# Hyena mixer: first loads in another order, and the last second-gate projections woven beside the long convolutions

## The chip, the core and the metric

One core of a Trainium2 chip runs the whole program once. The metric is device time in microseconds (us) of one execution. The engines that work on their own queues are PE (matrix products), DVE (vector), ACT (activations, casts, copies), POOL (a second, slower vector engine) and SP (which here only issues transfers). Each takes its instructions strictly in the order of its queue and waits on semaphores of the others.

## What is computed

Two blocks follow each other on a sequence of 512 positions and 1024 channels. The first has four layers, with mixers hyena, window attention, pooling, hyena, and a SwiGLU feed-forward behind each; the second is a gated delta network beside latent attention. The change lies for the most part in the first Hyena mixer, which is also the first work of the program:

```python
def hyena_mixer(xn, w_in, b_in, conv_w, conv_b, fw1, ..., w_out, b_out):
    u = short_conv(xn @ w_in + b_in)          # 3 x 1024 channels: x1, x2 (gates) and v
    kf = rfft(hyena_filters(...))             # sine MLP of 3 layers, a decay, a normaliser
    v = x1 * long_conv(v, kf[order 0])        # through a DFT
    v = x2 * long_conv(v, kf[order 1])
    return v @ w_out + b_out
```

(This is the reference cut down; xn is the RMS norm of x.) The normaliser is the sum of absolute filter values over time.

## The kernel before, in words

Everything is fp32, and a product of fp32 matrices is made of three matmuls on high and low parts (L384, L385, L386). A **part** is one projection of 128 output channels: 8 blocks of the contraction by 3 matmuls, so 24 matmuls of 128x512 into one PSUM bank. Its weights come as a raw tile `wraw` (L350), ACT casts the high half `whi` (L372) and DVE makes the low half `wlo` (L373).

The work of a stage is written as Python generators. `weave` (L205) takes, again and again, the next piece of the stream that has done the smallest share of its declared total, so the numbers `HY_IN`, `HY_F`, `HY_P` in line 232 set how the instructions of two streams lie between each other in each engine's queue. The queues are fixed when the program is built; nothing is reordered on the chip.

The first Hyena mixer runs in three stretches.

- **Start.** SP loads the eight tiles of x (L274), then weights, the DFT matrix `fwd` (L610) and the filter MLP's inputs (L556 to L566). ACT squares x (L446, L449), DVE adds the squares up (L450), PE sums over channels (L453), ACT and DVE make 1/rms (L456, L459). The filter MLP (`filter_mlp`, L553) is three small matmuls (L571), each followed by a chain of seven vector operations and a sine on ACT (L538 to L550).
- **Filters beside inputs.** `inputs` makes the 24 parts of w_in: four channel blocks q of 256 channels, three kinds (2 is v, 0 the first gate, 1 the second gate), two parts each. The evicted part is scaled, short-convolved (`short`: L790 on DVE, L792 on ACT, two L794 on DVE), transposed on PE (L802, not for kind 1) and stored to the DRAM tile `vd` by POOL (L806). Beside it `filters` makes eight filters (four blocks by two orders). Each has 16 matmuls L653, the normaliser (L665, `kacc` summed by POOL L661), the scaling (L667 to L672), the folds on POOL (L585, L586) and DVE (L595, L596), 16 DFT matmuls (L605), the scaling into K (L684), and a store of K to the DRAM tile `kd` by POOL (L689). The trace has two records for each matmul of the DFTs, their inverses and L665.
- **Convolutions.** `hyena_conv` runs two chains, blocks 0 and 2, blocks 1 and 3. Each order of a block loads K (L850), folds v on POOL, does 16 DFT matmuls (L605), the products with K on DVE and POOL, and 16 inverse matmuls (L863 or L871). The output projection `out` (L384 to L386, from `acth`) begins when two blocks are through.

The second Hyena mixer makes its filters earlier, in another stage, and projects its inputs beside its convolutions.

Waits that the change touches: a convolution of block q starts when all inputs of block q are there (`given[0] <= q`), and the SP queue loads K after POOL's stores that used the same memory before.

Of the kernel before, what the change touches and what calls it, by code (L numbers as in the profile page):

```python
# [15 lines left out]
P = 128  # L16
D = 1024
T = 512
KD = D // P
# [212 lines left out]
HY_Q, HY_IN, HY_F, HY_P = 4, 125.0, 140.0, 125.0  # L232
# [4 lines left out]
class Builder:  # L237
    def __init__(self, ctx, tc, i, o):
# [13 lines left out]
        self.open_x(i["xT"])  # L252
# [15 lines left out]
    def open_x(self, src):  # L268
# [3 lines left out]
        self.xsum, self.xsums = None, 0  # L272
        for k in range(KD):
            self.nc.sync.dma_start(out=self.x[k], in_=src[k * P:(k + 1) * P, :])  # L274
# [278 lines left out]
    def filter_mlp(self, tl, s):  # L553
        nc, i = self.nc, self.i
        z = tl([P, T], "sh")
        nc.sync.dma_start(out=z[:66, :], in_=i["c_z"])  # L556
        vf = tl([P, 4], "vf")
        nc.sync.dma_start(out=vf, in_=i["vf"][:, 4 * s:4 * s + 4])
        ws = []
        for j in range(3):  # L560
# [3 lines left out]
            for d in range(2):  # L564
                src = i["hy_f_w1"][s] if j == 0 else i["hy_f_wi"][s, j - 1]
                nc.sync.dma_start(out=w[kk * d:kk * d + kk, 64 * d:64 * d + 64], in_=src)  # L566
            ws.append(w)
        h, kk = z, 66
        for j in range(3):
# [4 lines left out]
            yield 8.0  # L574
# [38 lines left out]
    def filters(self, pool, s, ctl=None, nk=1):  # L613
# [133 lines left out]
    def hyena(self, li, s):  # L747
        self.vd = self.dram.tile([4, 3, P, 1024], F32, name=self.nm("vd"))
        with self.pool("hd") as dp:
            tl = self.tl(dp)  # L750
            with self.pool("hp") as pool:
                first = None
                if s in self.kd:
                    inputs = self.hyena_in(pool, pool, li, s)
                    self.fwd = self.load_dft(tl, "fwd")
                else:
                    with self.pool("hf") as fp:
                        inputs = self.hyena_in(pool, fp, li, s)
                        weave((inputs(0, HY_Q), HY_IN), (self.filters(fp, s, tl, 2), HY_F))
                        first = [tl([P, 4, 256], f"first{k}") for k in (2, 0)]  # L760
                        for t, k in zip(first, (2, 0)):
                            self.nc.sync.dma_start(out=t, in_=self.vd[0, k].rearrange("p (a c) -> p a c", a=4))
                if first is None:
                    with self.pool("hy") as pool:
                        self.hyena_conv(pool, s, first, inputs)
            if first is not None:
                with self.pool("hy") as pool:
                    self.hyena_conv(pool, s, first, inputs)
# [1305 lines left out]
```

## Time and profile before

| what | value |
|---|---|
| median of 3 runs | 4196.17 us (4184.2 to 4198.35) |
| profiled execution | 4197.38 us |
| its span | 4195.6 us |
| mean granted clock of PE | 0.966 of full speed |
| PE busy | 3970.3 us, 95% of the span |
| DVE, ACT, POOL busy | 60%, 37%, 23% |

The span is the time from the first to the last instruction; 1.8 us lie around it. A busy matmul row is not a matmul at full speed: the clock that the throttle grants PE has two levels, and at the lower one the same matmul takes about twice as long. So a stretch is read by three things together: how much of it PE was busy, at which clock, and what ended the idle time before an instruction (the releaser, behind `<-`).

### The profile page before, as it was taken

The numbers are of one execution on the slowest core, as the hardware profiler recorded it, in microseconds if no ns is written. First come the engines' busy times: TensorE is split into PE (matmuls) and PEld (weight loads), VectorE is DVE, ScalarE is ACT, GpSimd is POOL, SyncE is SP. The second block draws the span as 40 slices with busy tenths as digits, with TensorE's granted clock in tenths as the row PEclk, the third lists the DMA queues.
The fourth block names the chain that finished last, engine by engine and source line by source line (L and its number), as shares of the span: only waits on it lengthen the run. The fifth ranks groups of instructions, "written<-read, shape, count | busy, mean of one in ns | idle before, by whom it ended". The sixth has DMA issues, their size and how long they took to land. (4 is left out here: it accounts for less than half of the span.)

```text
span 4195.6 us, 48459 instructions
## 1 busy us (share of the span) xinstructions
PE 3970.3 (95%) x18340; PEld 3207.3 (76%) x18340; DVE 2502.2 (60%) x4113; ACT 1564.7 (37%) x2859; POOL 979.7 (23%) x1031
## 2 busy tenths in 40 slices
PE   7988999999999999999998999979999999999999
PEld 5777788876788777877877788768888876677887
DVE  6756887467634465556666544567767665644333
ACT  4321322258522352323222322454544456743222
POOL 2544211021101112323333110123333321102111
PEclk8999999999999999999999999989989989999999
DMA  4542355230232233434431323311112111242322
GB/s 155 171 175 97 101 190 191 86 108 31 71 100 92 83 106 119 132 117 151 154 123 63 100 93 99 94 56 51 56 59 63 56 45 45 91 136 81 100 91 91
DMA packets 370771, 421.83 MB, mean 101 GB/s; under 512 B 20614, under 2 KB 337046, under 8 KB 365674
## 3 DMA queue, kind: packets, MB, share of 16 engines
q1 hardware_dynamic: 361514, 377.46, 28.4%
q0 software_dynamic: 8736, 40.93, 2.6%
q8 instruction: 144, 2.36, 0.2%
q14 instruction: 89, 0.73, 0.1%
q10 hardware_dynamic: 288, 0.34, 0.0%
HBM read 372.27 MB, written 44.32 MB: 99 GB/s over the span
## 5 line engine op out<-in xcount | busy, mean ns | idle before, releaser
L372 ACT CAST whi<-wraw 128x1024 fp32r<-128x1024 f32 (+4 forms) x546 | 533.1, 977 | 1383.5 <-PE ps L385 1235.4
L384 PE MATMUL ps<-xh,whi 128*128 128x512 f32 x1904 | 784.8, 412 | 15.0 <-ACT whi L372 15.0
L373 DVE TENSOR_TENSOR wlo<-wraw,whi 128x1024 fp32r<-128x1024 f32 (+4 forms) x546 | 673.2, 1233 | 194.0 <-ACT whi L372 174.4
L386 PE MATMUL ps<-xh,wlo 128*128 128x512 f32 x1904 | 758.6, 399 | 2.5 <-DVE wlo L373 2.3
L385 PE MATMUL ps<-xl,whi 128*128 128x512 f32 x1904 | 755.2, 397 | 0.5 <-DVE xl L471 0.5
L384 PEld LDWEIGHTS ps<-xh,whi 128*128 128x128 f32 x1904 | 359.8, 189 | 99.7 <-ACT whi L372 15.5
L386 PEld LDWEIGHTS ps<-xh,wlo 128*128 128x128 f32 x1904 | 359.0, 189 | 94.0 <-DVE wlo L373 5.5
L385 PEld LDWEIGHTS ps<-xl,whi 128*128 128x128 f32 x1904 | 359.9, 189 | 88.2 <-issue 3.8
L527 POOL TENSOR_TENSOR u<-u,a 128x512 f32<-128x512 f32 x88 | 154.3, 1756 | 1011.2 <-ACT whi L372 720.7
L384 PE MATMUL ps<-hh,whi 128*128 128x512 f32 x960 | 385.0, 401 | 3.0 <-ACT hh L312 3.0
L386 PE MATMUL ps<-hh,wlo 128*128 128x512 f32 x960 | 380.6, 397 | 1.1 <-DVE wlo L373 1.1
L385 PE MATMUL ps<-hl,whi 128*128 128x512 f32 x960 | 380.2, 396 | 1.0 <-DVE hl L313 1.0
L384 PE MATMUL ps<-act,whi 128*128 128x512 f32 x656 | 278.4, 424 | 0.2 <-ACT whi L372 0.2
L386 PE MATMUL ps<-act,wlo 128*128 128x512 f32 x656 | 272.3, 415 | 0.5 <-DVE wlo L373 0.5
L385 PE MATMUL ps<-act,whi 128*128 128x512 f32 x656 | 272.5, 415 | 0.0
L384 PEld LDWEIGHTS ps<-hh,whi 128*128 128x128 f32 x960 | 181.2, 189 | 46.4 <-ACT hh L312 4.7
L386 PEld LDWEIGHTS ps<-hh,wlo 128*128 128x128 f32 x960 | 181.0, 189 | 45.3 <-DVE wlo L373 2.0
L385 PEld LDWEIGHTS ps<-hl,whi 128*128 128x128 f32 x960 | 181.2, 189 | 45.0 <-DVE hl L313 2.4
L532 DVE TENSOR_TENSOR x<-x,ps 128x512 f32<-128x512 f32 x128 | 87.7, 685 | 198.2 <-PE ps L386 197.8
L605 PE MATMUL ps<-pg,fwd 128*128 128x256 f32 x512 | 133.5, 409 | 30.1 <-DVE pg L595 30.1
L386 PEld LDWEIGHTS ps<-act,wlo 128*128 128x128 f32 x656 | 129.6, 197 | 29.9 <-DVE wlo L373 1.0
L385 PEld LDWEIGHTS ps<-act,whi 128*128 128x128 f32 x656 | 129.6, 198 | 25.1 <-issue 0.5
(539 smaller groups left out, 7238.7 us busy)
## 6 DMA issues: line engine op xcount, KB each, us to landing
wraw<-ff_w_gate SPq DMA_DIRECT2D x44, 1024.0 KB
wraw<-ff_w_up SPq DMA_DIRECT2D x44, 1024.0 KB
wraw<-ff_w_down SPq DMA_DIRECT2D x32, 1024.0 KB
wraw<-w_in SPq DMA_DIRECT2D x53, 512.0 KB
wraw<-hy_w_in SPq DMA_DIRECT2D x24, 1024.0 KB
w<-w_mod SPq DMA_DIRECT2D x24, 1024.0 KB
kd<-K POOLq DMA_DIRECT2D x16, 1152.0 KB, 4.7
K<-kd SPq DMA_DIRECT2D x16, 1152.0 KB
```

The source lines that it names most:

```text
L372: nc.scalar.copy(out=hi, in_=src)
L373: nc.vector.tensor_tensor(out=lo, in0=src, in1=hi.bitcast(F32), op=SUB)
L384: nc.tensor.matmul(out[:m, :cols], lhsT=whi[:, k, :m], rhs=xhi[:, :cols], start=(first and k == 0), stop=False)
L385: nc.tensor.matmul(out[:m, :cols], lhsT=whi[:, k, :m], rhs=xlo[:, :cols], start=False, stop=False)
L386: nc.tensor.matmul(out[:m, :cols], lhsT=wlo[:, k, :m], rhs=xhi[:, :cols], start=False, stop=(last and k == nk - 1))
L527: nc.gpsimd.tensor_tensor(out=u, in0=u, in1=a, op=MUL)
L532: self.nc.vector.tensor_tensor(out=self.x[j], in0=self.x[j], in1=ps, op=ADD)
L605: nc.tensor.matmul(ps[:, c, :], lhsT=self.fwd[:, t, s, c, :], rhs=st[t][s], start=(s == 0), stop=(s == 1))
```

## The change

- **Start.** The loads of x are split off from the tiles' allocation (`load_x`). In the first mixer the filter MLP is started first (`next(filters)`), and for it the MLP's loads go out on ACT's queue. Then come the first weight tile, now in two halves of 128 columns, the eight loads of x, and the other weights; `fwd` is loaded after the MLP's inputs. The squares go through `final(k)`: ACT squares, POOL adds (one buffer `xsq`), DVE adds the last.
- **Inputs.** Kind 1 of blocks 2 and 3 (two items, four parts, 96 matmuls) is taken out of the filter stretch and made by the stream `project` beside the convolutions, with a total of `HY_LATE` = 60. A convolution waits only for the items it needs. `HY_IN` goes from 125 to 104, `HY_F` from 140 to 148, the MLP's piece from 8 to 20.
- **Delay.** The eviction and short convolution of a part (`take`) is written one part later, in both Hyena mixers, and with it the transposes.
- **Second block.** One weight of the weave at the start of the delta network goes from 30 to 20.

The diff, cut:

```diff
-HY_Q, HY_IN, HY_F, HY_P = 4, 125.0, 140.0, 125.0
+LATE, HY_LATE = (2,3), 60.0
+HY_Q, HY_IN, HY_F, HY_P = 4, 104.0, 148, 125.0
...
     def filter_mlp(self, tl, s):
         nc, i = self.nc, self.i
+        q = nc.sync if s else nc.scalar
         z = tl([P, T], "sh")
-        nc.sync.dma_start(out=z[:66, :], in_=i["c_z"])
+        q.dma_start(out=z[:66, :], in_=i["c_z"])
...
-            yield 8.0
+            yield 20.0 if s == 0 else 8.0
...
+        yield from self.filter_mlp(tl, s)
         self.fwd = self.load_dft(ctl, "fwd")
-        yield from self.filter_mlp(tl, s)
...
-                self.want_cols(w, 0, KD, (kind * 8 + q * 2) * P, 256)
+                if s or kind != 1 or q not in LATE:
+                    self.want_cols(w, 0, KD, (kind * 8 + q * 2) * P, 256, 256 if self.plan else P)
+        for q in () if s else LATE:
+            self.want_cols(w, 0, KD, (8 + q * 2) * P, 256)
...
+            early = [(q, k) for q in range(4) for k in (2, 0, 1) if k != 1 or q not in LATE]
+            with self.pool("hp") as pool, self.pool("hf") as fp:
+                filters = self.filters(fp, s, tl, 2)
+                next(filters)
+                self.load(0)
+                self.load_x(self.i["xT"])
+                self.ahead()
+                inputs = self.hyena_in(dp, pool, fp, li, s)
+                for k in range(KD):
+                    self.final(k)
+                weave((inputs(early), HY_IN), (filters, HY_F))
...
+            with self.pool("hp2") as pool, self.pool("hy") as hy:
+                self.in_tiles = self.tl(pool)
+                self.hyena_conv(hy, s, first, inputs, [(q, 1) for q in LATE])
...
+        def inputs(items):
+            for q, kind in items:
+                st = self.in_tiles([P, 1024], "st", 2)
+
+                def consume(j, ps):
+                    given.append((j, ps, q, kind, st))
+                    if len(given) > 1:
+                        take(*given.pop(0))
+                yield from self.proj(2, xs, consume)
+            take(*given.pop())
+            turn(*waiting.pop())
...
-            while given[0] <= q:
+            while missing & {(q, 2), (q, 0)}:
                 yield 0.5
...
                 if order:
+                    while (q, 1) in missing:
+                        yield 0.5
...
-        weave((chain(conv(0), conv(2)), 76.0), (chain(conv(1, 12.0), conv(3)), 88.0), (out(0), 70.0), (project(), HY_P))
+        weave((chain(conv(0), conv(2)), 76.0), (chain(conv(1, 12.0), conv(3)), 88.0), (out(0), 70.0), (project(), HY_LATE if first else HY_P))
...
-        weave((self.gate_scalars(b2, lambda: tl([P, 6, P], "w", 7).rearrange("p c d -> p (c d)"), given[0], sc), 30),
+        weave((self.gate_scalars(b2, lambda: tl([P, 6, P], "w", 7).rearrange("p c d -> p (c d)"), given[0], sc), 20.0),
```

What this does to the queues stands below at two places; the names are those of the program, and the line numbers of the changed kernel are some 3 to 20 higher.

ACT's queue at the start, before:

```order
L254 DMA vecs<-vecs 128x542
L256 DMA ident<-c_ident 128x128
L446 ACT_TABLE_LOAD
L446 ACTIVATE tmp_221<-x_72 128x512
L470 ACTIVATE xh_108<-x_72,vecs 128x512
```

and in the changed kernel:

```order
L255 DMA vecs<-vecs 128x542
L257 DMA ident<-c_ident 128x128
L560 DMA sh_101<-c_z 66x512
L562 DMA vf_103<-vf 128x4
L570 DMA fw_19_105<-hy_f_w 33x64 x2
L570 DMA fw_20_109<-hy_f_wi 64x64 x2
L570 DMA fw_21_113<-hy_f_wi 64x64 x2
L375 ACT_TABLE_LOAD
L375 CAST whi_142<-wraw_130 128x1024
L473 ACTIVATE xh_152<-x_72,vecs 128x512
```

Eight more transfers are issued ahead of ACT's first computation, and the first cast of weights stands ahead of the first use of x. On PE the first small matmul of the filter MLP is now the first instruction, the second follows 13 projection matmuls later (before: 24 projection matmuls, the first, 24 more, the second), and the first normaliser matmul L665 (now L669) follows after 144 projection matmuls, before after 120. Between two normalisers stand 42 to 48 projection matmuls, before 60.

PE's queue where the last filter ends and the first convolution begins, before (`pg` and `S` are the folded inputs of a DFT, `xh` projects inputs, `inv` is an inverse DFT):

```order
L384 MATMUL ps_2089<-xh_136,whi_2023 128x512
L385 MATMUL ps_2089<-xl_137,whi_2023 128x512
L386 MATMUL ps_2089<-xh_136,wlo_2024 128x512
L605 MATMUL ps_2164<-pg_2160,fwd_168 128x256 x4
L605 MATMUL ps_2175<-pg_2161,fwd_168 128x256 x4
L605 MATMUL ps_2186<-S_2157,fwd_168 128x256 x4
L605 MATMUL ps_2197<-S_2157,fwd_168 128x256 x4
L863 MATMUL ps_2209<-pg_2169,inv_2155 128x256 x4
```

and in the changed kernel (of the projection matmuls, which come in threes, the first of some stand here):

```order
L609 MATMUL ps_1966<-S_1897,fwd_470 128x256 x4
L609 MATMUL ps_1972<-pg_1903,fwd_470 128x256 x4
L609 MATMUL ps_1978<-S_1897,fwd_470 128x256 x4
L609 MATMUL ps_1984<-pg_1904,fwd_470 128x256 x4
L609 MATMUL ps_2017<-pg_2013,fwd_470 128x256 x4
L387 MATMUL ps_2033<-xh_152,whi_1853 128x512
...
L609 MATMUL ps_2046<-pg_2014,fwd_470 128x256 x4
L387 MATMUL ps_2033<-xh_168,whi_1853 128x512
...
L609 MATMUL ps_2063<-S_2010,fwd_470 128x256 x4
```

Before, the last projection stands ahead of the first DFT of a convolution (`pg_2160`). Now the 16 DFT matmuls of the last filter run with nothing between, and the 96 late projections lie between the DFTs and inverses of the first order of blocks 0 and 1, up to the first DFT of the second order.

POOL's queue at the same place, before:

```order
L806 DMA vd_98<-st_1861 128x1024
L788 COPY q_2132<-nb_141 128x1
L789 COPY q_2132<-nb_141 128x1
L688 MEMSET K_2050 1x256
L689 DMA kd_167<-K_2050 128x2304
L806 DMA vd_98<-st_2022 128x1024
L585 TENSOR_TENSOR S_2157<-first_478_2144 128x512
```

and in the changed kernel:

```order
L820 DMA vd_90<-st_1574 128x1024
L820 DMA vd_90<-st_1773 128x1024
L692 MEMSET K_1923 1x256
L802 COPY q_2196<-nb_185 128x1
L803 COPY q_2196<-nb_185 128x1
L802 COPY q_2280<-nb_185 128x1
L803 COPY q_2280<-nb_185 128x1
L693 DMA kd_100<-K_1923 128x2304
L589 TENSOR_TENSOR S_2010<-first_459_1994 128x512
```

The store of the last filter is still ahead of the first fold of the convolution; the last store of inputs now stands ahead of the filter's.

## Rows read from the trace of the kernel before

**Rows 1.** The profile page, part 1: busy time, share of the span, instructions.
```profile
PE 3970.3 (95%) x18340; PEld 3207.3 (76%) x18340; DVE 2502.2 (60%) x4113; ACT 1564.7 (37%) x2859; POOL 979.7 (23%) x1031
```

**Rows 2.** Busy time by window: window, its length, PE, PEld, DVE, ACT, POOL, PEclk, DMA.
```profile
0.00:50.00 50.00, 30.70 (x110) 22.25 (x111) 37.47 (x61) 24.19 (x32) 4.24 (x14) 0.93 0.54 180
...
100.00:150.00 50.00, 46.62 (x226) 38.66 (x224) 36.64 (x50) 17.46 (x30) 26.50 (x32) 1.00 0.48 161
...
300.00:350.00 50.00, 41.85 (x167) 34.34 (x168) 32.03 (x48) 2.93 (x5) 28.27 (x34) 0.90 0.34 128
```

**Rows 3.** PE's timeline at the start: start, duration, engine, line, operation, idle before and releaser.
```profile
14.54 0.79 PE L384 MATMUL ps<-xh,whi 128*128 128x512 f32 x1 [14.54 <-ACT whi L372]
...
19.02 0.39 PE L385 MATMUL ps<-xl,whi 128*128 128x512 f32 x1
...
22.05 0.40 PE L386 MATMUL ps<-xh,wlo 128*128 128x512 f32 x1
...
34.54 2.08 PE L571 MATMUL ps<-sh,fw 128*128 128x512 f32 x2 [4.72 <-ACT sh L550]
```

**Rows 4.** ACT's timeline at the start: the issue of a transfer.
```profile
1.16 0.46 ACTq L256 DMA_DIRECT2D ident<-c_ident  x1
```

**Rows 5.** The normaliser line L665: duration ns, first and last start; four records to a filter.
```profile
L665 PE MATMUL ps<-kacc,ones x32: 378/379/795, 70.0 to 253.4; 128*128 128x256 f32 x32
```

**Rows 6.** PE's timeline in one filter: normaliser and folded DFT.
```profile
150.03 1.13 PE L665 MATMUL ps<-kacc,ones 128*128 128x256 f32 x4 [0.82 <-POOL kacc L661]
...
161.54 1.99 PE L605 MATMUL ps<-S,fwd 128*128 128x256 f32 x8 [0.70 <-POOL S L586]
...
175.21 1.03 PE L665 MATMUL ps<-kacc,ones 128*128 128x256 f32 x4
```

**Rows 7.** DVE's timeline in the same filter.
```profile
151.57 1.74 DVE L669 RECIPROCAL krs<-ps 128x256 f32<-128x256 f32 x1
...
163.42 0.68 DVE L790 TENSOR_TENSOR q<-ps,rstd 128x512 f32<-128x512 f32 x1
164.02 1.21 DVE L373 TENSOR_TENSOR wlo<-wraw,whi 128x1024 fp32r<-128x1024 f32 x1
165.15 0.74 DVE L794 SCALAR_TENSOR_TENSOR pc<-q,vecs,pc 128x512 f32<-128x512 f32 x1
```

**Rows 8.** PE's timeline where the convolutions begin.
```profile
276.02 1.89 PE L605 MATMUL ps<-pg,fwd 128*128 128x256 f32 x8
...
286.79 6.09 PE L605 MATMUL ps<-pg,fwd 128*128 128x256 f32 x16 [7.48 <-DVE pg L595]
```

**Rows 9.** POOL's timeline there.
```profile
279.17 0.53 POOL L689 DMA_DIRECT2D kd<-K  x1 [7.58 <-issue]
282.88 0.53 POOL L806 DMA_DIRECT2D vd<-st  x1 [3.17 <-DVE st L794]
```

**Rows 10.** SP's timeline there.
```profile
286.04 0.34 SPq L850 DMA_DIRECT2D K<-kd  x1
```

**Rows 11.** PE's timeline in the convolutions.
```profile
301.92 3.63 PE L605 MATMUL ps<-pg,fwd 128*128 128x256 f32 x8 [2.14 <-DVE pg L595]
...
321.39 2.25 PE L863 MATMUL ps<-pg,inv 128*128 128x256 f32 x8 [1.58 <-POOL pg L701]
326.95 6.48 PE L605 MATMUL ps<-pg,fwd 128*128 128x256 f32 x16 [3.30 <-DVE pg L595]
333.27 3.62 PE L605 MATMUL ps<-S,fwd 128*128 128x256 f32 x16
...
339.95 3.69 PE L605 MATMUL ps<-pg,fwd 128*128 128x256 f32 x16 [1.34 <-DVE pg L595]
...
357.90 3.75 PE L605 MATMUL ps<-pg,fwd 128*128 128x256 f32 x8 [3.90 <-DVE pg L595]
```

**Rows 12.** PE's waits from 240 to 410 us: total, times, longest.
```profile
PE ps L605 <- DVE pg L595: 21.7, 6, 7.5
```

**Rows 13.** PE's timeline at the start of the delta network.
```profile
2734.71 1.54 PE L1493 MATMUL ps<-ident,c 128*128 128x128 f32 x6 [6.64 <-ACT c L1485]
```

More of the change, by code (lines that the diff above doesn't have):

```diff
@@ L750, in hyena @@
             tl = self.tl(dp)
[L751 to L754, printed above, removed]
+            if s in self.kd:
+                with self.pool("hp") as pool:
+                    inputs = self.hyena_in(pool, pool, pool, li, s)
                     self.fwd = self.load_dft(tl, "fwd")
[L756 to L763, printed above, removed]
-                    with self.pool("hy") as pool:
-                        self.hyena_conv(pool, s, first, inputs)
@@ L766, in hyena @@
-            if first is not None:
-                with self.pool("hy") as pool:
-                    self.hyena_conv(pool, s, first, inputs)
-    def hyena_in(self, pool, fp, li, s):
+                    with self.pool("hy") as pool:
+                        self.hyena_conv(pool, s, None, inputs, [(q, k) for q in range(4) for k in (2, 0, 1)])
+                return
+            early = [(q, k) for q in range(4) for k in (2, 0, 1) if k != 1 or q not in LATE]
[9 more added lines that the diff above has]
+                weave((inputs(early), HY_IN), (filters, HY_F))
+                first = [tl([P, 4, 256], f"first{k}") for k in (2, 0)]
+                for t, k in zip(first, (2, 0)):
+                    self.nc.sync.dma_start(out=t, in_=self.vd[0, k].rearrange("p (a c) -> p a c", a=4))
@@ L806, in turn, with take, hyena_conv @@
                 nc.gpsimd.dma_start(out=self.vd[q, kind], in_=st)
[L808 to L821 removed]
+                self.in_done((q, kind))
+        def take(j, ps, q, kind, st):
+            r = None if kind == 1 else self.in_tiles([P, T], "pc", 2)
+            short(kind * 8 + q * 2 + j, ps, st[:, j * T:(j + 1) * T] if kind == 1 else r)
+            if waiting:
+                turn(*waiting.pop())
+            waiting.append((q, kind, st, j, r))
+        def inputs(items):
[8 more added lines that the diff above has]
+            turn(*waiting.pop())
         return inputs
[L824 removed]
+    def hyena_conv(self, pool, s, first, inputs, items):
         self.pgn = 12
@@ L834, in load @@
             return t
-        given = [HY_Q if first else 0]
+        missing = set(items)
+        self.in_done = missing.discard
         def project():
-            while given[0] < 4:
-                yield from inputs(given[0], given[0] + 1)
-                given[0] += 1
+            yield from inputs(items)
         def conv(q, lag=0.0):
             yield lag
-            while given[0] <= q:
+            while missing & {(q, 2), (q, 0)}:
                 yield 0.5
@@ L1998, in merge @@
             run(self.proj(8, ys, gdn))
-            self.open_x(xd)
+            self.open_x()
+            self.load_x(xd)
             run(self.proj(8, os, mla))
```

32 lines of the change are left out of this document (11 added, 21 removed).

## The prediction, made before the changed kernel had run

> **What bounds the kernel now.** I read the page first: PE is busy 95% of the span [rows 1], so over the whole program only PE's work, its clock or its idle time can be saved. The work hardly changes (the same matmuls, in another order), so the question is where PE idles or runs at its lower clock near the change. The windows show it: in the first 50 us PE is busy 30.7, between 100 and 150 us 46.6 at a granted clock of 1.00, between 300 and 350 us 41.9 at 0.90 [rows 2]. So the filter stretch is nearly full, and the start and the convolutions are not.
>
> PE's timeline of the start gives the first matmul at 14.54, behind the first cast of weights, and a wait of 4.72 for the first sine at 34.54 [rows 3]. From 19.02 to 22.05 lie 13 equal steps: 0.233 us for a projection matmul at full clock, so a part of 24 is 5.6 us.
>
> In the filter stretch the normaliser L665 marks the period: its first record starts at 70.0, the last at 253.4, of which about 0.7 is the last group itself [rows 5]. So the eighth group begins at 252.7, and seven periods take 182.7, 26.1 each. One of them shows both legs: normaliser at 150.03 after a wait of 0.82 for POOL, folded DFT at 161.54 after 0.70 for POOL, next normaliser at 175.21 without a wait [rows 6]. The waits are short: here PE's work and the chain through DVE and POOL are nearly even.
>
> In the convolutions it is the chain that leads: 21.7 us of PE's waits between 240 and 410 us are for DVE's fold, in six pieces [rows 12], and the lower clock follows the longer ones. After a wait of 2.14 eight records take 3.63, where the same eight take 1.89 behind no wait; after 3.30 sixteen take 6.48 against 3.62; after 1.34 they take 3.69, at full clock [rows 8, 11].
>
> **The change part by part.** *Start.* The filter MLP's first matmul stood behind the first part, which ends at 22.05 [rows 3]; now it is first on PE. I let it run at about 9, when its transfers have landed: 13 earlier. Against that, eight more issues stand at the head of ACT's queue, 0.46 each [rows 4], 3.7 in all, and the sines now stand behind the casts of x and three squares; I take 4.4 of the 13 back. The first filter is 8.6 earlier, but 24 more projection matmuls, 5.6, stand ahead of its normaliser: net 3 earlier, so 67. Bounds: 8 earlier (the wait of 4.72 gone, and the 3.5 that a clock of 0.93 costs in 50 us), or 5 later (the 3.7 of issues, with the sine as late as before and the 5.6 partly in sight).
>
> By the issue row, moving the MLP's transfers buys SP's queue their 0.46 each and costs ACT the same. The Trainium skill, page "DMA: Bandwidth & Descriptors", section "Issuing engines are not separate DMA queues", says that initiating transfers on several engines saves only the sequencer's time. By that rule the whole move is worth some 3.7 us on SP and is paid on ACT; the start would then be a wash, and the sum 3 us smaller. My 3 earlier does not come from the other queue, it comes from the order on PE.
>
> *Filter stretch.* Between two normalisers stand 42 to 48 projection matmuls instead of 60: 12 to 18 fewer, 2.8 to 4.2 us of PE, 3.5 in the middle. DVE loses with each part 0.68 + 1.21 + 2 x 0.74 = 3.4 [rows 7]. The leg from normaliser to folded DFT (11.5) is a chain of a reciprocal of 1.74 [rows 7], the subtraction and POOL's folds, and stays. The other leg (13.7) held no wait and shrinks with PE's and DVE's queues. Of the 3.5 I let 0.8 come back as waits for POOL: 23.4 a period, as 26.1 - 3.5 + 0.8. Bounds: 22.1 (all 3.5 saved, and a little of the early periods' waits), and 26.1 (nothing). Seven periods: 163.8 instead of 182.7. The last normaliser falls at 67 + 163.8 = 230.8, 21.9 earlier.
>
> *Transition.* From the last normaliser to the first DFT of a convolution it took 286.79 - 252.7 = 34.1 [rows 5, 8], the last DFT of a filter at 276.02, POOL's store of K at 279.17 and the store of the last inputs, on which the first fold queued, at 282.88 [rows 8, 9]. SP's load of K waited for that store too, and was issued at 286.04 [rows 10]. Now there is no store of inputs between them. I set 11.5 for the leg to the folded DFT, 8.6 for its four groups (6.9 at full clock, and 1.7 because PE idles some 3.5 ahead of them), 1.6 until the store of K as from 277.6 to 279.17, and 3.9 from a store to the DFT, as from 282.88 to 286.79: 25.6. That is 8.5 less; bounds 22 and 31. The first convolution begins at 256.4, 30.4 earlier.
>
> *Convolutions.* They get 96 matmuls, 22.4 us at full clock. What these can cover are the waits up to the second order: 2.14, 1.58 and 3.30, and the lower clock behind two of them, 3.63 - 1.89 = 1.74 and 6.48 - 3.62 = 2.86 [rows 11]; together 11.6. The waits of 1.34, 3.90 and another like it lie behind the last late matmul and stay. So this stage grows by 22.4 - 11.6 = 10.8. Bounds: 8 (also the slow first DFTs, 6.09 against 3.62 [rows 8]) and 22.4 (nothing covered).
>
> *The rest.* In the second Hyena evictions come a part later, with the next part's 5.6 us of PE work beside them: nothing, within 2 either way. At the start of the delta network ACT's silu now stands ahead of a table load and some gate work; the wait of 6.64 for it [rows 13] may lose some. I take 1 off; bounds 3 off and 3 on. Between the two blocks nothing moves.
>
> **Sum.** -30.4 + 10.8 - 1 = -20.6. The profiled execution was 4197.4; that gives 4176.8. The median of the runs stands 1.2 lower, so 4175.6: I say 4175. A difference of 0.3%, 12.6 us, is about what a measurement of this kernel can tell from no change.
>
> **The rivals.** *The filters' chain leads (0.17).* If POOL and DVE set both legs, the removed projections turn into waits and the periods stay at 26.1: the last normaliser at 67 + 182.7 = 249.7, and of the 20.6 there remain 1.7: 4194.5. For it speaks that PE already waited 0.82 and 0.70 for POOL at both ends of the first leg [rows 6]; against it that the second leg ended without a wait. Half of the effect gives 4185.
>
> What PE's clock does in that case goes with the rows of the convolutions: after 2.14 idle it fell, after 1.34 not [rows 11]. The Trainium skill, "TensorE: Matmul & The Clock Gate", section "What's actually happening", puts it that the throttled state is the default and that activity releases it. By that rule a stretch that ran at clock 1.00 is safe because it was full, and emptying it is a risk; the trace agrees as far as the clock falls behind idle time. If each of seven periods got one dip like that behind 2.14, it would cost 7 x 1.74 = 12.2 of the 20.6, and the time would be 4188; I count this into this rival.
>
> *The start comes late (0.11).* ACT's queue at the start holds eight issues, ten casts and squares paced by POOL ahead of the first sine. If PE waits for the second sine matmul with only 13 projection matmuls behind it instead of 48, it lacks 35 x 0.233 = 8.2 us of cover; the first normaliser comes at 75, and the time is 4184. For it: the present wait of 4.72 at the same place, with more cover [rows 3].
>
> *The convolutions get longer than they save (0.07).* PE takes its queue in order, so a late projection whose low weights are not ready holds up the DFT behind it. The DVE chain already leads there [rows 12], and gets four parts of 3.4, 13.5 us. If that falls in line with the folds, nothing is covered, and the late matmuls run at the lower clock (44.8 instead of 22.4), the stage grows by 58: with 30.4 won before, 4223. It turns against the change from the point where the stage grows by over 31 us. Against it: DVE is busy only 32.0 of 50 there [rows 2].
>
> That the parts do not really move is excluded: PE's queue shows them between the DFTs.
>
> **How the numbers follow.** My forecast has 0.65, with a range of its own from 4160 (periods of 22.1, and the good ends of the start) to 4184 (periods of 24.6). The rivals have 0.17, 0.11 and 0.07. Faster by over 0.3% is most of the forecast (0.60), a third of the late start and a quarter of the rival on the chain: 0.68. Slower by over 0.3% is the last rival, 0.06. The rest, 0.26, is the same. The range from 4157 to 4193 leaves out the last rival, the worst of the chain rival and some of the best ends.
>
> **What would show it.** Right: the first normaliser at 67 or earlier, periods near 23.4 with waits for POOL below 1 us at each leg, the first convolution DFT near 256, no store of inputs between the last K store and the first fold, the waits at the first order's ends gone, and the output projection 20 us earlier. Wrong: waits over 2 us in every period with a clock below 1.00 between 100 and 230 us; the second sine matmul later than 30; projection matmuls among the convolutions that wait for DVE.

## The result, and the profile after

The changed kernel is slower: a median of 4216.61 us (4205.7 to 4223.15, 7 runs) against 4192.63 (4179.92 to 4200.14, 7 runs), a ratio of 1.0060 with a 95% interval from 1.0048 to 1.0073. Forecast was 4175, with a range to 4193. The profiled execution has a span of 4212.1, 16.5 longer. The other 7.5 us of the difference of the medians are not placed by it. A second run of the same queues (e6 below) has a span of 4222.1, so a part of the difference varies from run to run.

Four landmarks of the first Hyena mixer show where its share goes. They are read from PE's timelines: the first and the eighth normaliser, the first DFT of a convolution, the first matmul of the output projection.

| us | before | after | forecast | stretch before | stretch after | change |
|---|---|---|---|---|---|---|
| first normaliser | 69.96 | 78.76 | 67 | 69.96 | 78.76 | +8.8 |
| eighth normaliser | 252.63 | 254.40 | 230.8 | 182.67 | 175.64 | -7.0 |
| first convolution DFT | 286.79 | 280.79 | 256.4 | 34.16 | 26.39 | -7.8 |
| first output projection | 380.86 | 393.26 | about 361 | 94.07 | 112.47 | +18.4 |

Together +12.4. Through the rest of the first block the distance stays at 12.4. The second Hyena adds 3.2, and behind it less than 1 us lasts. In e6 the distances are 13.8 at the output projection, 6.6 more through the second Hyena and some 6 more behind it. So most of the loss that the trace places lies where the prediction looked for the gain, and three of its four terms are wrong.

The windows of the changed kernel:

```profile
0.00:50.00 50.00, 29.06 (x86) 19.52 (x87) 34.92 (x50) 22.32 (x30) 10.30 (x16) 0.88 0.52 169
...
100.00:150.00 50.00, 45.87 (x222) 37.80 (x221) 42.91 (x50) 17.06 (x28) 29.67 (x30) 1.00 0.46 153
...
200.00:250.00 50.00, 42.13 (x207) 35.37 (x207) 32.95 (x46) 15.93 (x26) 25.86 (x30) 1.00 0.45 153
...
300.00:350.00 50.00, 43.76 (x195) 36.64 (x194) 39.36 (x53) 7.18 (x11) 27.04 (x33) 0.98 0.43 153
```

Against [rows 2], the start has less of PE and a lower clock (0.88, it was 0.93). From 300 to 350 us PE has more to do at a better clock, but DVE rose from 32.0 to 39.4. The clock between 100 and 150 us is 1.00 as before: the filter stretch did not lose its clock, it got waits (for POOL's fold `S` and for the normaliser's sum `kacc`). PE's waits from 100 to 250 us, of the kernel before:

```profile
PE ps L605 <- POOL S L586: 3.8, 6, 1.3
PE ps L665 <- POOL kacc L661: 2.6, 4, 0.8
```

and of the changed one:

```profile
PE ps L609 <- POOL S L590: 10.1, 6, 2.1
PE ps L669 <- POOL kacc L665: 6.3, 3, 3.1
```

Between the first and the eighth normaliser stand 324 projection matmuls, where there were 408 (48 in the first period before, 60 in the others). The 84 are 19.6 us of PE. The stretch got 7.0 shorter; most of the rest is waiting, 16.4 instead of 6.4 in this window alone. The normaliser's rows, which answer to [rows 5], and those of e6, the same queues run again:

```profile
L669 PE MATMUL ps<-kacc,ones x32: 379/379/796, 78.8 to 255.2; 128*128 128x256 f32 x32
```

```profile
L669 PE MATMUL ps<-kacc,ones x32: 379/379/796, 76.1 to 256.9; 128*128 128x256 f32 x32
```

In e6 the stretch takes 180.0, only 2.6 less than before. Of the 19.6 us, then, 3 to 7 were saved.

PE's timeline of the start, which answers to [rows 3]:

```profile
8.67 2.05 PE L575 MATMUL ps<-sh,fw 66*128 66x512 f32 x2 [8.67 <-DMA fw<-hy_f_w]
12.62 0.79 PE L387 MATMUL ps<-xh,whi 128*128 128x512 f32 x1 [1.91 <-ACT xh L473]
...
21.17 0.79 PE L388 MATMUL ps<-xl,whi 128*128 128x512 f32 x1 [3.15 <-DVE xl L474]
...
24.91 2.08 PE L575 MATMUL ps<-sh,fw 128*128 128x512 f32 x2 [2.09 <-ACT sh L553]
...
41.92 1.02 PE L575 MATMUL ps<-sh,fw 128*128 128x512 f32 x2
...
48.62 1.11 PE L816 MATMUL ps<-ident,pc 128*128 128x128 f32 x4 [4.28 <-DVE pc L808]
...
78.76 1.65 PE L669 MATMUL ps<-kacc,ones 128*128 128x256 f32 x3 [7.35 <-POOL kacc L665]
```

The first sine matmul runs 13.6 us earlier, at 8.67, the second 9.6 earlier, the third only 0.6 earlier: at 41.92, where it was at 42.51. The first matmul of a filter, which needs the third sine, runs 6.0 later, and PE comes to it without a wait, where it waited 2.57 before. Before:

```profile
59.34 0.64 PE L653 MATMUL ps<-w3h,sa 128*128 128x256 f32 x2 [2.57 <-ACT w3h L312]
```

and after:

```profile
65.31 0.28 PE L657 MATMUL ps<-w3h,sa 128*128 128x256 f32 x1
```

The last 2.8 of the 8.8 come behind it, on the way to POOL's sum, for which PE waits 7.35 (3.68 before).

In the convolutions the late matmuls cover the waits of 2.14 and 1.58 of [rows 11] and most of that of 3.30, and a longer one comes behind them:

```profile
280.79 3.78 PE L609 MATMUL ps<-pg,fwd 128*128 128x256 f32 x8 [5.09 <-DVE pg L599]
...
333.34 1.97 PE L609 MATMUL ps<-pg,fwd 128*128 128x256 f32 x8 [0.53 <-DVE pg L599]
...
349.32 6.63 PE L609 MATMUL ps<-pg,fwd 128*128 128x256 f32 x16 [5.71 <-DVE pg L599]
...
370.20 3.75 PE L609 MATMUL ps<-pg,fwd 128*128 128x256 f32 x8 [3.89 <-DVE pg L599]
```

The wait of 3.30 at 326.95 is now 0.53. That of 1.34 at 339.95, ahead of the second order of block 1, is now 5.71, and the clock falls behind it: sixteen records take 6.63, before 3.69. DVE's timeline ahead of it:

```profile
337.06 0.68 DVE L804 TENSOR_TENSOR q<-ps,rstd 128x512 f32<-128x512 f32 x1
337.65 1.52 DVE L376 TENSOR_TENSOR wlo<-wraw,whi 128x512 fp32r<-128x512 f32 x1
...
340.29 0.73 DVE L808 SCALAR_TENSOR_TENSOR st<-q,vecs,st 128x512 f32<-128x512 f32 x1
...
341.55 0.73 DVE L808 SCALAR_TENSOR_TENSOR st<-q,vecs,st 128x512 f32<-128x512 f32 x1
...
344.01 5.16 DVE L599 SCALAR_TENSOR_TENSOR pg<-S,vx 128x512 f32<-128x512 f32 x1
```

and POOL's:

```profile
342.82 0.57 POOL L820 DMA_DIRECT2D vd<-st  x1
...
346.15 1.25 POOL L589 TENSOR_TENSOR S<-vx 128x512 f32<-128x512 f32 x1
347.37 1.25 POOL L590 TENSOR_TENSOR S<-vx 128x512 f32<-128x512 f32 x1
```

In the kernel before POOL began this fold at:

```profile
337.99 1.27 POOL L585 TENSOR_TENSOR S<-vx 128x512 f32<-128x512 f32 x1
```

The eviction and short convolution of the last late part, with a tile of low weights between them 3.7 us, stand on DVE among the products of block 0. POOL adds these products, four pairs of them, and stores the late gate before it folds block 1, so the fold ends at 348.6; DVE's record of 5.16 is mostly a wait for it. Before, the fold stood behind three pairs and no store.

### The profile page after: what moved, and what is told of

Its sections match the earlier page's. It is cut to its first block, busy times and chain, and to the rows that moved or that the text cites. A ratio compares the mean times of both kernels' runs of the same rounds, so it can differ in the third digit from the quotient of the medians.

```text
span 4212.1 us, 48469 instructions
## 1 busy us (share of the span) xinstructions
PE 3969.3 (94%) x18340; PEld 3205.8 (76%) x18340; DVE 2520.5 (60%) x4107; ACT 1565.0 (37%) x2858; POOL 989.6 (23%) x1037
## 5 line engine op out<-in xcount | busy, mean ns | idle before, releaser
L376 DVE TENSOR_TENSOR wlo<-wraw,whi 128x1024 fp32r<-128x1024 f32 (+4 forms) x546 | 681.7, 1249 | 207.3 <-ACT whi L375 186.6
L387 PEld LDWEIGHTS ps<-act,whi 128*128 128x128 f32 x656 | 129.2, 197 | 25.2 <-ACT whi L375 0.6
```

The source lines that it names most:

```text
L376: nc.vector.tensor_tensor(out=lo, in0=src, in1=hi.bitcast(F32), op=SUB)
L387: nc.tensor.matmul(out[:m, :cols], lhsT=whi[:, k, :m], rhs=xhi[:, :cols], start=(first and k == 0), stop=False)
```

## The experiments

Each comparison is with the kernel before on the same chip. "After" is 1.0060 (1.0048 to 1.0073). The landmarks are of one profiled execution each, and repeat to a few us: the changed kernel's queues, run again (e6), gave 76.1 and 256.2 for the normalisers (78.8 and 254.4), those of the kernel before (e7) 71.1 and 252.1 (70.0 and 252.6). The time of e6 is 1.0044 (1.0027 to 1.0060). None of the edits below that were to ease something is clear of it in the time, so the traces have to rank them.

| run | ratio, 95% interval | first norm. | eighth | conv. DFT | output |
|---|---|---|---|---|---|
| e1 start as before | 1.0079 (1.0067 to 1.0091) | 73.7 | 249.9 | 292.2 | 403.1 |
| e2 no late parts | 1.0056 (1.0044 to 1.0069) | 86.2 | 273.1 | 301.5 | 391.7 |
| e3 no delay | 1.0080 (1.0065 to 1.0094) | 83.0 | 270.8 | 300.5 | 410.4 |
| e4 late parts alone | 1.0061 (1.0046 to 1.0076) | 69.3 | 245.8 | 286.2 | 397.7 |
| e5 frame alone | 1.0012 (1.0003 to 1.0020) | 69.9 | 253.0 | 288.4 | 380.6 |
| e8 late total 42 | 1.0034 (1.0022 to 1.0046) | 75.4 | 252.9 | 280.9 | 383.7 |
| e9 reciprocal behind | 1.0037 (1.0023 to 1.0051) | 75.2 | 251.4 | 280.3 | 389.5 |
| e11 more late parts | 1.0041 (1.0028 to 1.0054) | 72.2 | 242.2 | 271.1 | 383.7 |
| e13 less vector work | 1.0035 (1.0023 to 1.0047) | 74.5 | 252.7 | 280.7 | 391.1 |
| e15 MLP closer | 1.0066 (1.0043 to 1.0089) | 65.9 | 234.2 | 281.9 | 393.7 |
| e16 two K buffers | 1.0046 (1.0030 to 1.0061) | 75.6 | 247.0 | 273.8 | 383.2 |
| e17 all eased | 1.0047 (1.0029 to 1.0065) | 75.9 | 252.2 | 281.4 | 384.3 |

### Which part of the change

**Start as before.** Edit, of the changed kernel:

```diff
-                next(filters)
-                self.load(0)
-                self.load_x(self.i["xT"])
-                self.ahead()
...
-                for k in range(KD):
-                    self.final(k)
```

with x loaded at its allocation, the MLP's loads on SP behind `fwd`, its piece 8 and undivided first weights.

> The changed kernel with its start put back: x is loaded first, the filter MLP's transfers stand on SP behind the weights and the DFT matrix, its first matmul stands behind the first part, and the squares are summed by DVE. Late parts, delay and the weight in the second block stay. Theory 1 (the start lost the time: its first normaliser came at 78.8 us in the profile, before at 70.0): the first normaliser comes at 70 or earlier, and the time falls by about 9 us, to some 4207. Rival (the start is hidden, since the filter stretch is bound by its own chain and the late parts cost the time in the convolutions): the normaliser comes earlier, but the first DFT of a convolution stays within 3 us of 280.8 and the time stays within 4 us of 4216.

Both missed. The time rose. The first normaliser came at 73.7, but with 96 matmuls ahead of it instead of 144, and PE had waited 10.2 for the first filter weights at 63.2. The changed start as such is not where the whole loss is.

**No late parts:**

```diff
-LATE, HY_LATE = (2,3), 60.0
-HY_Q, HY_IN, HY_F, HY_P = 4, 104.0, 148, 125.0
+LATE, HY_LATE = (), 60.0
+HY_Q, HY_IN, HY_F, HY_P = 4, 125.0, 140.0, 125.0
```

> The changed kernel with no late parts: all 24 parts are projected beside the filters, with the weights of that weave as before (125 and 140). Start, delay and second block stay as changed. Theory 1 (the start and the delay lost the time): slower than the kernel before by what these two cost, 9 + 3, so some 12 us over it, with the first normaliser near 79 or later and the last near 262. Rival (the late parts lost it, 18 us of growth in the convolutions against 6 won ahead of them): within 4 us of the kernel before, and the stretch from the first DFT of a convolution to the output projection back at 130 us.

Not the rival: 1.0056, some 23 us, twice what theory 1 allowed. The convolution stretch is short again (90.2 us), and the filters are long: the first normaliser stands behind 192 matmuls, and the periods are 26.7. Start and delay without the late parts lose as much as everything together, so the losses do not add.

**No delay:**

```diff
                 def consume(j, ps):
-                    given.append((j, ps, q, kind, st))
-                    if len(given) > 1:
-                        take(*given.pop(0))
+                    take(j, ps, q, kind, st)
                 yield from self.proj(2, xs, consume)
-            take(*given.pop())
```

> The changed kernel with eviction and short convolution written directly behind their part again, in both Hyena mixers. Theory (the delay costs where transposes wait for it: 3.4 us in the second Hyena, and waits of 4.3 and 5.1 us of PE for the short convolution at 48.6 and 266.0 us): faster than the changed kernel by 3 to 10 us, and these two waits shrink. Rival (the waits only change places, PE then waits for POOL's folds): within 3 us of the changed kernel in the first Hyena, 3.4 less in the second.

Missed on the other side: slower than the changed kernel, by 17 us at the output projection (in the time the intervals just overlap). With this start the delay helps; without it the periods are 26.8 and the first normaliser comes at 83.0.

**Late parts alone** (the edits of the first and third experiment together, and 30 again in the second block):

> Only the late parts: start, delay and the weight in the second block are as in the kernel before, the weave of the filter stretch has the changed weights (104 and 148). Theory 1 (the late parts as such win a little, start and delay lose it): first DFT of a convolution near 272 us, stretch of the convolutions longer by 18, so the first Hyena within 4 us of the kernel before, and the whole within 5 us of it. Rival (late parts lose by themselves, because the filter stretch does not get shorter when matmuls leave it): 10 us or more slower than the kernel before.

The rival. The start is the old one (69.3), yet the filter stretch takes 176.5, 6.2 less than before, with mostly 48 matmuls a period, as in the changed kernel, the 66 early matmuls that are left (48 before) run in a transition of 40.4, and the convolutions grow to 111.5. So the late parts lose 1.0061 by themselves.

**Frame alone** (those edits, and that of the second):

> The changed kernel with all named parts undone: no late parts, start, delay, weave weights and the weight in the second block as before. What is left is the frame: the other nesting of the pools (the scale and offsets of the inputs outlive the filters) and the rule by which a convolution waits only for the two kinds of input that it folds. The first three experiments each undid one part, and none gave the time back. Theory A (the parts interact, each alone loses in its own place): within 6 us of the kernel before, 4 to 6 of them in the second Hyena. Theory B (the frame itself loses the time): 15 us or more over the kernel before, with the loss in the first Hyena.

Theory A by the time: the pools and the new waiting rule cost 0.1%, at most 0.2%. The trace does not place this loss: its span is that of the kernel before (4195.7 and 4195.6), and the second Hyena is 1.3 longer, not 4 to 6.

### The convolutions

**A smaller total for the late parts:**

```diff
-LATE, HY_LATE = (2,3), 60.0
+LATE, HY_LATE = (2,3), 42.0
```

> The changed kernel with a total of 42 instead of 60 for the late parts, so that they lie closer together and end earlier in the first order of the convolutions. In the profile of the changed kernel PE waits 5.71 for DVE's fold at 349.3, and that fold waits for POOL's, which stands behind products that DVE finishes late because a late part's four DVE instructions (some 3.6 us) are among them. Theory (the tail of the late parts causes this wait): the wait at this place falls below 3 us, and the lower clock behind it goes; 4 to 7 us faster than the changed kernel. Rival (the wait is the chain's own): it stays above 5, and the time within 3 us of the changed kernel.

The wait went as the theory said, but not in the way it said. `weave` takes the stream that has done the smallest share of its total, so a smaller total makes the turns of a stream rarer: the late parts lie further apart here, and not denser. Their last matmul, in the changed kernel:

```profile
336.31 0.40 PE L389 MATMUL ps<-xh,wlo 128*128 128x512 f32 x1
```

and here, with POOL's store of the last late gate (342.82 in the changed kernel) and its fold of block 1:

```profile
350.42 0.39 PE L389 MATMUL ps<-xh,wlo 128*128 128x512 f32 x1
```

```profile
337.09 1.27 POOL L589 TENSOR_TENSOR S<-vx 128x512 f32<-128x512 f32 x1
...
359.51 0.57 POOL L820 DMA_DIRECT2D vd<-st  x1 [1.24 <-DVE st L808]
```

PE's waits from 278 to 385 us are now these four:

```profile
280.87 3.58 PE L609 MATMUL ps<-pg,fwd 128*128 128x256 f32 x8 [5.09 <-DVE pg L599]
326.30 3.69 PE L609 MATMUL ps<-pg,fwd 128*128 128x256 f32 x16 [0.56 <-DVE pg L599]
360.97 3.75 PE L609 MATMUL ps<-pg,fwd 128*128 128x256 f32 x8 [4.98 <-DVE pg L599]
377.61 3.75 PE L609 MATMUL ps<-pg,fwd 128*128 128x256 f32 x8 [3.54 <-DVE pg L599]
```

The wait of 5.71 with its low clock is gone, and that of 3.89 is now 4.98. Two things changed at this place. POOL's fold stands behind three pairs of additions again, as before the change, and 22 late matmuls lie between the second orders of blocks 0 and 1, where the changed kernel has 6. A late part's DVE instructions still stand among the products (331.43 to 335.84), so that they alone make the wait is not shown; which of the two took it away was not separated. The stretch is 102.8 instead of 112.5: it grew by 8.7 over the kernel before, inside the forecast's bounds of 8 and 22.4. The output projection comes 9.6 earlier than in the changed kernel and 11.0 earlier than in e6. The ratio fell from 1.0060 to 1.0034, 10.9 us, but only 4 us below that of e6: the gain is shown by the traces, its size in the time is not.

### The filter stretch

**Reciprocal behind** the subtraction, in DVE's queue. A first try that only exchanged the two statements (e6, and e7 on the kernel before, at 1.0000) left the queues as they were, so both are repeats. Then, with a copy of one element on ACT that makes the reciprocal wait for the subtraction:

```diff
-        nc.vector.reciprocal(out=rs[:, 0, :], in_=ps)
         od = tl([P, 4, 256], "od", 1)
...
+        nc.scalar.copy(out=rs[0:1, 0, 0:1], in_=od[0:1, 0, 0:1])
+        nc.vector.reciprocal(out=rs[:, 0, :], in_=ps)
```

> The changed kernel with the reciprocal really behind the subtraction in DVE's queue (in the run called reciprocal later the builder had put it back, so that run repeated the changed kernel): a copy of one element by ACT makes it wait for the subtraction. The leg from normaliser to folded DFT loses 1.7 us on DVE; the copy adds work to ACT alone. Theory 1 (the filter stretch is bound by this chain once the matmuls are gone): the leg falls from 11.4 to about 9.7, PE's waits of 2.1 for the fold nearly vanish, periods from 25.1 to about 23.5, and the time falls by 8 to 14 us. Rival (DVE and POOL together bind, and what leaves one leg comes back in the other): periods stay above 24.6 and the time within 4 us of 4216.

The rival by the periods; the time fell by 9.6 us against the first measurement of the changed kernel, as theory 1 had it, and by 3 against e6, as the rival had it. PE's waits from 100 to 250 us:

```profile
PE ps L669 <- POOL kacc L665: 16.2, 5, 4.3
```

Those for the fold (10.1) are gone, those for the normaliser's sum went from 6.3 to 16.2, the sum of both from 16.4 to 16.2. Periods: 25.2. But the edit moved more than the reciprocal. In DVE's queue of the changed kernel a product `k`, on which the normaliser's sum depends, and a tile of low weights stand ahead of the wait for POOL's fold:

```profile
183.87 0.68 DVE L659 TENSOR_TENSOR k<-ps,dec 128x512 f32<-128x512 f32 x1
184.47 1.45 DVE L376 TENSOR_TENSOR wlo<-wraw,whi 128x1024 fp32r<-128x1024 f32 x1
189.71 0.69 DVE L599 SCALAR_TENSOR_TENSOR pg<-pg,od 128x512 f32<-128x512 f32 x1 [3.79 <-POOL pg L596]
```

and in this run behind it:

```profile
184.13 0.69 DVE L599 SCALAR_TENSOR_TENSOR pg<-pg,od 128x512 f32<-128x512 f32 x1 [3.75 <-POOL pg L596]
...
185.34 0.68 DVE L659 TENSOR_TENSOR k<-ps,dec 128x512 f32<-128x512 f32 x1
185.94 1.22 DVE L376 TENSOR_TENSOR wlo<-wraw,whi 128x1024 fp32r<-128x1024 f32 x1
```

DVE waits 26.3 us for that fold between 70 and 256 us, where it waited 17.7. So the run does not tell whether the freed time went to the next link by itself or by this new order. The same edit in the kernel before:

> The kernel before with the same edit. With 60 matmuls a period PE waited only 0.7 for the fold, and then led. Theory 1: 0 to 5 us faster than the kernel before, less than half of what the same edit does to the changed kernel. Rival: the same gain in both, 8 us or more, or none in both.

1.0002 (0.9993 to 1.0011), periods 26.1 as before: no gain there.

**More late parts:**

```diff
-LATE, HY_LATE = (2,3), 60.0
-HY_Q, HY_IN, HY_F, HY_P = 4, 104.0, 148, 125.0
+LATE, HY_LATE = (1,2,3), 60.0
+HY_Q, HY_IN, HY_F, HY_P = 4, 93.6, 148, 125.0
```

> The changed kernel with the second gate of block 1 made late too: 18 parts beside the filters, 6 beside the convolutions (144 late matmuls), 42 projection matmuls to a period where there were 48. Theory 1 (chain-bound filters): the periods fall by less than 0.5 us though 1.4 us of PE's work leave each, PE's waits grow by the rest, and the convolutions grow by most of the 11.2 us of the two parts: 6 to 12 us slower than the changed kernel. Rival (PE's work sets the period): periods fall by 1.4 us, 10 us in all, and the time stays within 4 us of the changed kernel or falls.

Between the two. Periods fell by 0.8 for 1.4 us of PE less, the eighth normaliser came 12.2 earlier than in the changed kernel, and the convolution stretch up to the output projection was no longer than there (112.6). But the feed-forward begins at 496.3, as in the changed kernel (496.1): what was won ahead was lost between the output projection's first matmul and its end.

**Less vector work:**

```diff
-            for j in (1, 2):
+            for j in ((1, 2) if s or n in (12, 13, 14, 15) else (1,)):
```

> The changed kernel without the third tap of the short convolution in the 20 early parts of the first mixer: one DVE instruction of 0.74 us less for each part, PE's and POOL's work untouched (so the output is another). Theory 3 (DVE's queue, in order, with its waits for POOL's folds, sets the filter period; the last kacc waits for a product that stands behind other DVE work): two parts to a period, so periods 1.0 to 1.5 us shorter than 25.1, and the eighth normaliser 7 to 10 us earlier counted from the first. Rival (POOL's or PE's own queue sets it): periods within 0.4 of 25.1.

> The kernel before without the same tap in the same 20 parts (the four parts of the second gate of blocks 2 and 3 keep it). Theory 3 with PE close behind: 2.5 parts to a period take 1.8 us from DVE, but PE's 60 matmuls hold 25 us a period, so the periods fall from 26.1 only to about 25. If DVE alone sets them, they fall to 24.3; if PE alone, they stay within 0.3.

The output of these two kernels is another one; they serve the trace alone. Theory 3 failed in this form. The first four periods are 0.8 shorter than in the changed kernel and in e6, short of the 1.0 to 1.5. The last three are longer, 27.1 to 28.2, and DVE's timeline there shows why:

```profile
184.59 0.41 DVE L316 TENSOR_TENSOR w3l<-sh,w3h 128x256 fp32r<-128x256 f32 x1
188.66 0.69 DVE L688 TENSOR_TENSOR K<-ps,krs 128x512 f32<-128x512 f32 x1 [3.66 <-DMA kd<-K]
189.27 0.68 DVE L659 TENSOR_TENSOR k<-ps,dec 128x512 f32<-128x512 f32 x1
```

The scaling into K waits at the head of DVE's queue until the store of the last K has landed, since there is one K buffer, and the product `k` stands behind it. That the missing tap brought this out is not shown: e6, the changed kernel's own queues, has it too, with last periods of 25.6, 28.7 and 27.1:

```profile
220.40 0.69 DVE L688 TENSOR_TENSOR K<-ps,krs 128x512 f32<-128x512 f32 x1 [3.41 <-DMA kd<-K]
...
247.53 0.69 DVE L688 TENSOR_TENSOR K<-ps,krs 128x512 f32<-128x512 f32 x1 [3.10 <-DMA kd<-K]
```

The kernel before with the tap left out: 1.0004 (0.9994 to 1.0013), periods 25.8 against 26.1, the branch in which PE alone sets them.

**Two K buffers** in the first mixer:

```diff
-        K = tl([P, 9, 256], "K", 1)
+        K = tl([P, 9, 256], "K", 1 if s else 2)
```

> The changed kernel with two buffers instead of one for the scaled filter K in the first mixer. In the run with less vector work DVE waited 11.0 us (three times, up to 3.8) until POOL's store of the last K had landed, at the head of its queue, and its last three periods were 27.1 to 28.2; in the changed kernel it waits 3.0 us, twice. Theory 4 (a ring of short waits between PE, DVE, POOL and the store sets the period, each link a few us): the wait for the store is gone, the periods from 177 to 254 us fall by 0.5 to 1.5, the eighth normaliser by 2 to 4 us, the time by 0 to 5. Rival (the store does not matter): the periods stay within 0.2.

Theory 4: the last three periods are 24.3, 24.3 and 23.9, where the changed kernel has 25.6, 25.5 and 25.8, and e6 25.6, 28.7 and 27.1. DVE has no wait for the store left. The eighth normaliser comes 7.4 earlier, 4.3 of it counted from the first, and the output projection 10.1. In the time, 1.0046 (1.0030 to 1.0061), it does not show.

**All links eased** (two K buffers, the reciprocal behind, `HY_LATE` 42):

> The changed kernel with all links eased at once: two K buffers, the reciprocal behind the subtraction, denser late parts (42). Theory 4: freeing one link moved the wait to the next, freeing several lets the period fall towards PE's own work of some 22 us; periods near 24, the first Hyena level with the kernel before, the time 4193 to 4203. If another link (the normaliser's sum on POOL) takes over, the periods stay near 25.2 and the time near 1.003 of the kernel before.

The other branch: from 100 to 250 us PE waits 17.1 for POOL's sum and no longer for the fold, periods 25.2. They are longer than the 24.5 of two K buffers alone, so in these traces the reciprocal's new place costs instead of easing. The same without the second K buffer (e12) gave 1.0032 (1.0020 to 1.0044), with periods of 25.0; it had been forecast level with the kernel before if the two gains added up. The kernel before with two K buffers and the later reciprocal is at 1.0003 (0.9992 to 1.0015); no version beat both kernels.

**MLP closer:**

```diff
-            yield 20.0 if s == 0 else 8.0
+            yield 8.0
```

> The changed kernel with 8 instead of 20 as the filter MLP's piece, as before: the weave then puts 72 instead of 144 projection matmuls ahead of the first normaliser, and 120 instead of 42 between the last one and the first inverse DFT. Theory (the start is a chain of sines that DVE, ACT and the low clock hold up, not PE's matmuls): though 16.8 us of PE's work leave, the first normaliser comes only 5 to 9 us earlier than 78.8, so that the whole loses: 4 us or more slower than the changed kernel. Rival (PE's matmuls set it): 14 us or more earlier, and the whole within 4 us of the changed kernel or faster.

Between: 12.9 earlier than in the changed kernel, 9 to 11 than in most other runs with its start, for 16.8 us of PE less. Here PE does wait for the first filter weights, and takes them 9.9 earlier than the changed kernel does:

```profile
55.45 0.80 PE L657 MATMUL ps<-w3h,sa 128*128 128x256 f32 x2 [11.55 <-ACT w3h L315]
```

So with 144 matmuls ahead of the normaliser it is PE's queue that comes late to the filters, with 72 it is the weights. The periods are 24.0 with nearly the same number of matmuls as in the changed kernel (318 for 324). The time is that of the changed kernel (1.0066).

## Why the prediction was wrong

- **The step that failed most is "Of the 3.5 I let 0.8 come back as waits for POOL".** Both numbers are off. The 84 matmuls' 19.6 us are 2.8 a period and not 3.5: most periods lose 12, only one 18, and the first 6 (it had 48 before and not 60). Of these 2.8, 1.0 was saved and 1.8 came back, in e6 0.4 and 2.4. The forecast for seven periods was -18.9, the traces give -7.0 and -2.6. This is the first rival, that the filters' chain leads, for most of its price, but without the fall of the clock that was counted into it. I had read a leg that ends without a wait [rows 6] as room for PE. What seems to hold the period is a ring: normaliser, DVE, POOL's folds, DFT, scaling into K with its store, and, behind these in DVE's queue, the products for the next sum. One link is shown: a second K buffer (e16) took away the wait for the store and 1.2 to 1.9 us from each of the last three periods. That PE's load alone does not set the period is shown too: with nearly the same matmuls it is 25.1 in the changed kernel, 24.5 in e16, 24.0 in e15. That the rest is a closed ring is argued: e9 and e17, meant to show it, changed the order of DVE's queue as well. A full order of the links is open.
- **The start** was forecast 3 earlier and came 8.8 later, 2.2 to 7.2 in the eight other runs with the same start, the delay and 144 matmuls. The 13 for the first sine were right. The step "I take 4.4 of the 13 back" was not: 13.0 of the 13.6 were gone at the third sine matmul. It stands behind 66 projection matmuls, and before behind 67, so the new order could not bring it forward; PE comes to it without a wait. From there to the first filter matmul PE has 66 more, before 53, some of them behind a wait of 4.28 for the short convolution, and is 6.0 late; the last 2.8 come in the chain behind it. This was the rival on the late start, at the size it gave (75); its cause, PE lacking cover for the second sine, was not the one: PE waited 2.09 there.
- **The transition** was right: 25.6 forecast, 26.4 measured, and not by luck: 12.8 for the leg to the folded DFT (forecast 11.5), 13.6 from there to the first convolution (forecast 14.1), with no store of inputs between the last K store and the first fold.
- **The convolutions**: growth of 10.8 forecast, 18.4 measured. "The waits of 1.34, 3.90 and another like it lie behind the last late matmul and stay" is the step that failed: the first of them went from 1.34 to 5.71 and took the low clock with it, 7.3 together (4.4 and 2.9), because POOL's fold of the next order came to stand behind a fourth pair of additions and the store of the late gate. With it the sum comes out: 22.4 for the late matmuls, less the 11.6 covered but for 0.5, and 7.3 more, is 18.6. With the late parts further apart (e8) it was gone, and the growth was 8.7. Of the rival's 58 nothing more came true: the late matmuls ran at full clock but for the first few.
- **The second Hyena** was put at nothing, within 2; it is 3.2 longer (6.6 in e6), and 1.0 to 1.6 longer in the three runs without the delay. **The delta network** gave neither gain nor loss.
- The prediction's signs of being wrong were a second sine matmul later than 30, waits over 2 us with a clock below 1.00, and late matmuls that wait for DVE. None of the three came as described: the sine was at 24.91, and the waits came at full clock.
- The rule of the Trainium skill on issuing engines ("DMA: Bandwidth & Descriptors", "Issuing engines are not separate DMA queues") fits the start: ACT's eight issues end at 9.57, and its first cast runs at 10.90. The sum by that rule, 3 us smaller, would have missed as well.
- The clock stayed at 1.00 from 100 to 250 us in spite of waits up to 3.1 there, so no time was lost to it in that stretch. The rule of the Trainium skill that stands beside the first rival ("TensorE: Matmul & The Clock Gate", "What's actually happening") made emptying the stretch a risk; here it did not come to pass.

## What to carry to other kernels

Where an engine waits a few tenths at both ends of a leg, other engines are level with it; work taken from it can then come back as waits (here 13 to 17 of 19.6 us), while the place to which the work moves still charges for it (here 18.4 for 22.4 us of matmuls). Before moving work out of such a stretch, count what the other engines' chain would take, single buffers and stores included, and try the move on the vector engine's queue as well as on PE's. Count also what stands ahead of each step in the queue: a chain whose first step moves forward gains nothing where its last step keeps its place. Undoing one part at a time can mislead where parts were fitted to each other: the frame alone cost 0.1%, while taking any one part out of the whole gave no more than 0.04% back. And an edit should be read in the queues before its result is read: two edits here did something else than they were made for.

## What was not expected of the hardware

Additions and subtractions of DVE and POOL that run side by side slow each other. The low half of a weight tile takes 1.21 us on DVE [rows 7]; in the changed kernel it took 3.04 while POOL was folding, and POOL's instruction beside it 1.71, where the same one takes 0.74 in e9, without that tile beside it. It happened in three of the seven periods of the changed kernel, and no such tile of the filter stretch took over 1.70 in the kernel before. What it costs the period was not tested. DVE's timeline of the changed kernel, POOL's, and POOL's of e9:

```profile
158.94 3.04 DVE L376 TENSOR_TENSOR wlo<-wraw,whi 128x1024 fp32r<-128x1024 f32 x1
```

```profile
160.87 1.71 POOL L595 TENSOR_TENSOR pg<-od 128x256 f32<-128x256 f32 x1
```

```profile
180.15 0.74 POOL L595 TENSOR_TENSOR pg<-od 128x256 f32<-128x256 f32 x1
```
